# A state-space stage's small matmuls in groups of a few, with dense steps between the groups

## The chip, the cores and the metric

The kernel runs on one core of a Trainium2 chip. The metric is device time in microseconds (us), as the median of several executions. The engines are PE (TensorE: matmuls, with PEld for its weight loads), DVE (VectorE), ACT (ScalarE), POOL (GpSimd) and SP (SyncE, which here issues most transfers). Each engine works through its own list in order.

## What is computed

One layer of a decoder: four token mixers work on the same projection of the input, each is projected up to 1024 channels, gated and summed, and an output projection, a norm, an MLP and a second norm follow. The part that matters here is the state-space mixer (S5) and how it joins the sum:

```python
def _s5_mixer(u, ...):
    bu_re = jnp.einsum('bsgh,gph->bsgp', ug, bb_re)      # and bu_im
    _, _, x_re, x_im = lax.associative_scan(combine, (a_re, a_im, bu_re, bu_im), axis=1)
    y = (jnp.einsum('bsgp,ghp->bsgh', x_re, c_re) - jnp.einsum('bsgp,ghp->bsgh', x_im, c_im)
         + d * ug)
    y = jax.nn.gelu(y.reshape(bsz, s, BRANCH_WIDTH))
    return y * jax.nn.sigmoid(y @ glu_w + glu_b)

branches = (y_s5, y_fox, y_rwkv, y_sb)
merged = sum(jax.nn.sigmoid(gates[:, :, n]) * (branches[n] @ w_branch[i, n])
             for n in range(N_BRANCHES))
```

There are 1024 tokens, 1024 channels and 256 channels for each mixer; S5 has 16 groups of 16 channels with 64 complex states each.

## The kernel before

All large products are done in a split float32 (a high and a low part of each operand): a **dense step** is three matmuls of 128x512, `a*xh`, `a*xl` and `b*xh`, after which the function `dense` yields. Eight steps make one tile of a gate, two make one of a branch's up-projection. The steps of the gates and up-projections of all four branches stand one behind the other in the generator `merges`, in the order RWKV, FoX, S5, stick-breaking. I call it the dense stream; its tiles are named `mm` in the rows. While it runs, the FoX, S5 and stick-breaking mixers are computed one after the other as processes beside it (`attn`, `s5_tables` with `s5`, `attn` again); their PSUM tiles are named `x`.

PE's order is fixed when the program is built. `Driver.run` keeps a modelled time. In each round it lets a process whose time has come run up to its next `yield`, and only when none is due does it take the next step of the dense stream:

```python
ready = [p for p in self.procs if p[0] <= self.now]
if ready:
    ...
    p[0] = self.now + 0.2 if lat is None else self.mark + lat
    continue
if fill is not None:
    got = next(fill, "end")
```

So everything that a process gives to PE between two yields stands in one piece, and after a yield at least one dense step (0.645 us in that model) comes before the process goes on. Where the dense stream needs a branch that isn't finished, it answers "wait", and PE has only what the processes give. DVE's and ACT's lists are put in the order of the modelled times; SP's follows the order in which the code issues.

The S5 stage gives PE these pieces. In `s5_tables`: 16 small products `bd,Gm` (called L here; 128x32, each two matmul instructions), then 16 transposes `cst,Gm` into four PSUM tiles (GT). In `s5`, for each of two halves (`p4`): 32 products `U,GT`; a chain on DVE that ends in the state `X` (its two parts are written one after the other); then the Y products, for eight groups of channels one `U,Tg` and two `X,Hm` each (six matmul instructions of 128 columns), into two PSUM tiles, with a gelu on ACT and DVE after each tile. At the end, `yt` is read back from DRAM, eight products `yt,gw` are done, and the result (`ynat`) goes through ACT and DVE to DRAM (`scr_Y`). From there the dense stream loads it back as the operand `y` (four loads `wr<-scr_Y`, a cast on ACT and a subtraction on DVE for each), and the first step of the S5 branch's up-projection, `mm<-y`, reads it. The weights for that step are a chunk `wr<-in_w_branch`, cast by ACT to `vh`, with the rest `vl` from DVE. The stick-breaking stage begins when S5 has finished; it loads `raw` and `st` tiles on SP, and its first matmuls on PE are transposes `cst,st` and products `KH,QS`; its first transposes `cst,W` follow after a chain on ACT and DVE.

Of the kernel before, what the change touches and what calls it, by code (L numbers as in the profile page):

```python
# [316 lines left out]
def body(ctx, tc, I, O, dbg=None):  # L317
# [25 lines left out]
    def nm(s):  # L343
        uid[0] += 1
        return f"{s}_{uid[0]}"
# [15 lines left out]
    def px():  # L361
        return ps.tile([P, 512], F32, tag="x", name=nm("x"), bufs=5)
# [282 lines left out]
    def rwkv(pool, wa, g1, have, late, spare):  # L645
# [246 lines left out]
        def chain():  # L892
            St = pool.tile([P, 2, 64], F32, tag="St", name=nm("St"), bufs=3)
            V.memset(St, 0.0)
            for qt in range(4):
# [7 lines left out]
                for c_ in range(4):  # L903
# [13 lines left out]
                    yield 0.1  # L917
                    U = px()
                    for ct, hh, hd, hp in heads:
                        js = slice(hd * 64, hd * 64 + 64)  # L920
                        T.matmul(U[up, js], lhsT=TT[up, hd * 2 + c_ // 2, :], rhs=Xs[up, js], start=True, stop=True)
                    A.copy(VU[up, c_, :], U[up, 0:256])
                    V.tensor_tensor(out=sd, in0=St, in1=ec[:, :, c_:c_ + 1].to_broadcast([P, 2, 64]), op=ALU.mult)
# [219 lines left out]
    def tt(o, a, b, op):  # L1143
        V.tensor_tensor(out=o, in0=a, in1=b, op=op)
        return o
# [12 lines left out]
    def cmul(orr, oi, ar, ai, br, bi, tmpf):  # L1158
        a, b = tmpf(), tmpf()
        tt(a, ar, br, ALU.mult)  # L1160
        tt(b, ai, bi, ALU.mult)
        tt(orr, a, b, ALU.subtract)
        a, b = tmpf(), tmpf()
        tt(a, ar, bi, ALU.mult)
        tt(b, ai, br, ALU.mult)
        tt(oi, a, b, ALU.add)
# [103 lines left out]
    def s5_tables(pool):  # L1270
        pw, fr, fi = s5v["pw"], s5v["fr"], s5v["fi"]

        def small(shape, name):
            return pool.tile(shape, F32, tag="s2k", name=nm(name), bufs=4)
        bc_in = small([P, 4, 8, 16], "bcin")
        SY.dma_start(out=bc_in, in_=I["s5_bc"])
        br, bi, cr, ci = (bc_in[:, i] for i in range(4))
        dsb = small([P, 256], "dsb")
        G.dma_start(out=dsb, in_=I["s5_d"].partition_broadcast(P))
        zz = small([112, 256], "zz")  # L1280
        G.memset(zz, 0.0)
        SY.dma_start(out=SCR["L"][128:240], in_=zz)

        def t1k(shape=(P, 8, 8, 16)):
            return pool.tile(list(shape), F32, tag="t1k", name=nm("t1k"), bufs=2)
        E = pool.tile([P, 2, P, 8], F32, tag="E", name="E", bufs=1)
        V.memset(E[:, 0, 0, :], 1.0)
        V.memset(E[:, 1, 0, :], 0.0)

        def grow(k):  # L1290
            n = 1 << k
            bcs = [x.unsqueeze(1).to_broadcast([P, n, 8]) for x in s5v["steps"][k]]
            cmul(E[:, 0, n:2 * n, :], E[:, 1, n:2 * n, :], E[:, 0, 0:n, :], E[:, 1, 0:n, :], bcs[0], bcs[1],
                 lambda: t1k((P, 64, 8))[:, :n, :])

        def b16(a):
            return a.unsqueeze(2).to_broadcast([P, 8, 16])
        bb = pool.tile([P, 2, 8, 16], F32, tag="bb", name="bb", bufs=1)

        def t128():  # L1300
            return pool.tile([P, 8, 16], F32, tag="t128", name=nm("t128"), bufs=4)
        for k in range(5):
            grow(k)
            if k % 2:
                yield 0.1
        cmul(bb[:, 0], bb[:, 1], b16(fr), b16(fi), br, bi, t128)
        nci = pool.tile([P, 8, 16], F32, tag="nci", name="nci", bufs=1)
        ts(nci, ci, -1.0, ALU.mult)
        bd = pool.tile([P, 2, 8, 2, 16], F32, tag="bd", name="bd", bufs=1)
        G.memset(bd, 0.0)  # L1310
        for e in range(2):
            es = slice(e * 64, e * 64 + 64)
            for i, w in ((0, cr), (1, nci)):
                A.copy(bd[es, i, :, e, :], w[es])
        yield 0.1
        pwp = pw.rearrange("p i j a -> p i a j")
        Gm = pool.tile([P, 2, 8, 8, 16], F32, tag="a", name="Gm", bufs=1)
        Hm = pool.tile([P, 2, 8, 8, 16], F32, tag="Hm", name="Hm", bufs=1)

        def bj(a):  # L1320
            return a.unsqueeze(3).to_broadcast([P, 8, 8, 16])

        def bh(a):
            return a.unsqueeze(2).to_broadcast([P, 8, 8, 16])
        prev = [pwp[:, i, :, 7::-1] for i in range(2)]
        pnx = [pwp[:, i, :, 1:9] for i in range(2)]
        cmul(Gm[:, 0], Gm[:, 1], bj(prev[0]), bj(prev[1]), bh(bb[:, 0]), bh(bb[:, 1]), t1k)
        yield 0.1
        lo = px()
        for pr in range(8):  # L1330
            for i in range(2):
                T.matmul(lo[:, pr * 32:pr * 32 + 32], lhsT=Gm[:, i, pr].rearrange("p s h -> p (s h)"),
                         rhs=bd[:, i, pr].rearrange("p e h -> p (e h)"), start=i == 0, stop=i == 1)
        Ls = small([P, 256], "Ls")
        tt(Ls.rearrange("p (g h) -> p g h", h=16), dsb.rearrange("p (g h) -> p g h", h=16),
           cc("eye7").unsqueeze(1).to_broadcast([P, 16, 16]), ALU.mult)
        tt(Ls, Ls, lo[:, 0:256], ALU.add)
        SY.dma_start(out=SCR["L"][0:128], in_=Ls)
        GT = pool.tile([P, 2, 8, P], F32, tag="GT", name="GT", bufs=1)
        for i in range(2):  # L1340
            for p4 in range(2):
                o = px()
                for j in range(4):
                    T.transpose(o[:, j * P:(j + 1) * P], Gm[:, i, p4 * 4 + j].rearrange("p s h -> p (s h)"), ident)
                A.copy(GT[:, i, p4 * 4:p4 * 4 + 4, :].rearrange("p a b -> p (a b)"), o)
        U = pool.tile([P, 16, P], F32, tag="a", name="U", bufs=1)
        for s in range(8):
            SY.dma_start(out=U[s * 16:(s + 1) * 16], in_=SCR["u"].rearrange("(g h) s c -> s h g c", h=16)[s])
        a1, a2 = t1k(), t1k()
        tt(a1, bj(pnx[0]), bh(cr), ALU.mult)  # L1350
        tt(a2, bj(pnx[1]), bh(ci), ALU.mult)
        tt(Hm[:, 0], a1, a2, ALU.subtract)
        yield 0.1
        a1, a2 = t1k(), t1k()
        tt(a1, bj(pnx[0]), bh(nci), ALU.mult)
        tt(a2, bj(pnx[1]), bh(cr), ALU.mult)
        tt(Hm[:, 1], a1, a2, ALU.subtract)
        Tg = pool.tile([P, 16, 8, 16], F32, tag="Tg", name="Tg", bufs=1)
        for s in range(0, 8, 2):
            Tz = small([P, 2, 256], "Tz")  # L1360
            for i in range(2):
                SY.dma_start(out=Tz[:, i, :], in_=SCR["L"][(7 - s - i) * 16:(7 - s - i) * 16 + 128])
            A.copy(Tg[:, :, s:s + 2, :], Tz.rearrange("p s (g h) -> p g s h", h=16))
        for k in range(5, 7):
            grow(k)
            yield 0.1
        yield from s5(pool, GT, Tg.rearrange("p g s h -> p g (s h)"), Hm.rearrange("p i a s h -> p i a (s h)"),
                      E.rearrange("p i j a -> p i a j"), U)

    def s5(pool, GT_, Tg_, Hm_, E_, U_):  # L1370
        def tt(o, a, b, op):
            V.tensor_tensor(out=o, in0=a, in1=b, op=op)
# [7 lines left out]
        for p4 in range(2):  # L1380
            a4 = slice(p4 * 4, p4 * 4 + 4)
            GT, Hm, Ev = GT_[:, :, a4], Hm_[:, :, a4], E_[:, :, a4]
            Tg, U = Tg_[:, p4 * 8:p4 * 8 + 8], U_[:, p4 * 8:p4 * 8 + 8]
            Z = pool.tile([P, 2, 4, P], F32, tag="t1k", name=nm("Z"), bufs=2)
# [33 lines left out]
            for g4 in range(2):  # L1418
                o = px()
                for j in range(4):  # L1420
                    g = j * 2 + g4
                    pr, es = g // 2, slice((g % 2) * 64, (g % 2) * 64 + 64)
                    os_ = o[:, j * P:(j + 1) * P]
                    T.matmul(os_, lhsT=Tg[:, g], rhs=U[:, g, :], start=True, stop=False)
                    for i in range(2):
                        T.matmul(os_, lhsT=Hm[es, i, pr], rhs=X[es, i, pr, :], start=False, stop=i == 1)
                w = pool.tile([P, 512], F32, tag="s2k", name=nm("gl"), bufs=4)
                A.activation(out=w, in_=o, func=AF.Square)
                V.tensor_scalar(out=w, in0=w, scalar1=0.044715, scalar2=1.0, op0=ALU.mult, op1=ALU.add)
                tt(w, o, w, ALU.mult)  # L1430
                A.activation(out=w, in_=w, func=AF.Tanh, scale=math.sqrt(2.0 / math.pi))
                V.scalar_tensor_tensor(out=Ye[:, g4], in0=w.rearrange("p (a b) -> p a b", b=P), scalar=1.0,
                                       in1=o.rearrange("p (a b) -> p a b", b=P), op0=ALU.add, op1=ALU.mult)
# [818 lines left out]
```

## Time and profile before

| what | value |
|---|---|
| median of 3 executions | 1868.21 us (1867.77 to 1874.67) |
| the profiled execution | 1875.13 us, its span 1873.3 us |
| PE busy | 1816.4 us, 97% |
| DVE busy | 1237.8 us, 66% |
| ACT busy | 714.3 us, 38% |
| mean granted TensorE clock | 0.983 |

The span goes from the first to the last instruction; the execution's own time is 1.8 us longer. Busy PE means that some matmul is under way, at either of its two clock levels (2.4 GHz, shown as 1.00, and 1.2 GHz, shown as 0.50), so a busy share of 97% doesn't tell at which speed.

### The profile page before, as it was taken

What the parts mean: (1) busy time and instruction counts of PE and PEld (TensorE: products, weight loads), DVE (VectorE), ACT (ScalarE), POOL (GpSimd) and SP (SyncE); (2) the same over time, 40 slices, a digit from 0 to 9 for tenths busy, and PEclk for the clock granted to TensorE, in tenths of its full rate; (3) what the DMA queues carried; (4) which work ended last, traced back from release to release, by engine and by line L of the source; (5) the groups of instructions that cost most, each with busy time, mean ns of one, the idle gap of its engine ahead of it and who ended that gap; (6) DMA issues with size and microseconds to landing.
All of it is one profiled execution on the core that took longest, in us unless ns stands there. A gap on an engine that the chain in (4) does not pass through costs nothing. (4 is left out here: it accounts for less than half of the span.)

```text
span 1873.3 us, 27588 instructions
## 1 busy us (share of the span) xinstructions
PE 1816.4 (97%) x9651; PEld 1479.0 (79%) x9651; DVE 1237.8 (66%) x2596; ACT 714.3 (38%) x1412; POOL 206.9 (11%) x279
## 2 busy tenths in 40 slices
PE   8999999998999999999999998999999999999998
PEld 6877777777788877777877886788888887888876
DVE  7675855616876765688867667666656565866574
ACT  5443343215554212555544125343333343433230
POOL 0331111100000000000000001111121111111000
PEclk9999999999999988999999999999999999999999
DMA  7334223124422411412155118898989898988441
GB/s 254 108 123 112 76 81 95 63 69 139 146 90 78 104 38 50 137 54 67 44 197 160 62 57 234 239 254 223 255 235 251 212 268 256 284 212 229 127 147 48
DMA packets 178012, 275.27 MB, mean 147 GB/s; under 512 B 37824, under 2 KB 59616, under 8 KB 177744
## 3 DMA queue, kind: packets, MB, share of 16 engines
q1 hardware_dynamic: 155552, 226.31, 37.3%
q0 software_dynamic: 22320, 47.18, 12.8%
q8 instruction: 76, 1.25, 0.3%
q14 instruction: 64, 0.52, 0.1%
HBM read 199.76 MB, written 56.89 MB: 137 GB/s over the span
## 5 line engine op out<-in xcount | busy, mean ns | idle before, releaser
L327 PE MATMUL mm<-t,wh 128*128 128x512 f32 x1600 | 514.3, 403 | 3.8 <-ACT th L280 1.9
L327 PEld LDWEIGHTS mm<-t,wh 128*128 128x128 f32 x1600 | 293.8, 190 | 66.5 <-issue 2.4
L327 PE MATMUL mm<-t,wl 128*128 128x512 f32 x800 | 314.9, 394 | 0.0
L327 PE MATMUL x<-t,wp 128*128 128x512 f32 x1152 | 270.8, 394 | 14.1 <-DVE wp L280 6.8
L327 PEld LDWEIGHTS x<-t,wp 128*128 128x128 f32 x1152 | 217.7, 190 | 64.3 <-DVE wp L280 9.9
L327 PE MATMUL x<-sx,wp 128*128 128x512 f32 x768 | 179.6, 389 | 0.2 <-DVE wp L280 0.2
L327 PEld LDWEIGHTS mm<-t,wl 128*128 128x128 f32 x800 | 151.8, 190 | 33.4
L327 PEld LDWEIGHTS x<-sx,wp 128*128 128x128 f32 x768 | 144.1, 188 | 30.5 <-DVE wp L280 0.7
L280 ACT CAST wh<-wr 128x512 fp32r<-128x512 f32 (+1 forms) x125 | 74.5, 596 | 123.1 <-PE mm L327 90.7
L280 DVE TENSOR_TENSOR wp<-wr,wp 128x512 fp32r<-128x512 f32 x96 | 65.8, 687 | 77.2 <-ACT wp L280 77.2
L280 ACT CAST wp<-wr 128x512 fp32r<-128x512 f32 x96 | 59.1, 620 | 147.8 <-DMA wr<-wl 69.3
L280 POOL TENSOR_TENSOR wl<-wr,wh 128x512 fp32r<-128x512 f32 x50 | 67.7, 1353 | 280.6 <-ACT wh L280 280.4
L327 PE MATMUL mm<-t,wp 128*128 128x512 f32 x384 | 90.6, 392 | 0.0
L327 PE MATMUL mm<-sx,wp 128*128 128x512 f32 x384 | 89.6, 389 | 0.0
L327 PE MATMUL mm<-wo,t 128*128 128x512 f32 x384 | 89.0, 391 | 0.0
L327 PEld LDWEIGHTS mm<-t,wp 128*128 128x128 f32 x384 | 72.6, 189 | 15.6 <-DVE wp L280 0.4
L327 PEld LDWEIGHTS mm<-sx,wp 128*128 128x128 f32 x384 | 72.1, 188 | 14.9
L327 PEld LDWEIGHTS mm<-wo,t 128*128 128x128 f32 x384 | 71.6, 188 | 14.5
L280 DVE TENSOR_TENSOR wl<-wr,wh 128x512 fp32r<-128x512 f32 (+1 forms) x75 | 47.3, 633 | 40.4 <-ACT wh L280 39.5
L280 DVE TENSOR_TENSOR wp<-wl,wp 128x512 fp32r<-128x512 f32 x64 | 43.7, 687 | 42.5 <-ACT wp L280 42.5
L280 DVE TENSOR_TENSOR wp<-wh,wp 128x512 fp32r<-128x512 f32 x64 | 43.9, 689 | 33.7 <-ACT wp L280 33.7
L280 ACT CAST wp<-wl 128x512 fp32r<-128x512 f32 x64 | 39.3, 620 | 50.0 <-DMA wl<-wr 16.5
(380 smaller groups left out, 3199.4 us busy)
## 6 DMA issues: line engine op xcount, KB each, us to landing
wr<-in_w_in_dram SPq DMA_DIRECT2D x110, 256.0 KB
scr_H<-sn SPq DMA_DIRECT2D x100, 256.0 KB
wr<-in_mlp_w_dram SPq DMA_DIRECT2D x84, 256.0 KB
sn<-scr_H SPq DMA_DIRECT2D x84, 256.0 KB
wh<-in_mlp_w_dram SPq DMA_DIRECT2D x56, 256.0 KB
wl<-in_mlp_w_dram SPq DMA_DIRECT2D x56, 256.0 KB
wr<-wl POOLq DMA_DIRECT2D x32, 256.0 KB, 6.5
wl<-wr POOLq DMA_DIRECT2D x32, 256.0 KB, 4.7
```

What stands on the lines that cost most here:

```text
L280: r = f(*a, **kw)
L327: return nc.tensor.matmul(out, lhsT=lhsT, rhs=rhs, **kw)
```

## The change

Three bare `yield None` are added: one after each of the eight pairs of L products, one after each of the four tiles of GT transposes, and one after each group of Y products.

```diff
@@ s5_tables
             for i in range(2):
                 T.matmul(lo[:, pr * 32:pr * 32 + 32], lhsT=Gm[:, i, pr].rearrange("p s h -> p (s h)"),
                          rhs=bd[:, i, pr].rearrange("p e h -> p (e h)"), start=i == 0, stop=i == 1)
+            yield None
         Ls = small([P, 256], "Ls")
@@ s5_tables
                     T.transpose(o[:, j * P:(j + 1) * P], Gm[:, i, p4 * 4 + j].rearrange("p s h -> p (s h)"), ident)
                 A.copy(GT[:, i, p4 * 4:p4 * 4 + 4, :].rearrange("p a b -> p (a b)"), o)
+                yield None
         U = pool.tile([P, 16, P], F32, tag="a", name="U", bufs=1)
@@ s5
                     T.matmul(os_, lhsT=Tg[:, g], rhs=U[:, g, :], start=True, stop=False)
                     for i in range(2):
                         T.matmul(os_, lhsT=Hm[es, i, pr], rhs=X[es, i, pr, :], start=False, stop=i == 1)
+                    yield None
                 w = pool.tile([P, 512], F32, tag="s2k", name=nm("gl"), bufs=4)
```

The dense stream itself keeps its order and its number of steps. What moves is where the S5 and stick-breaking pieces stand in it.

PE at the first half's Y products, before. The row in front is the last dense matmul; each group is one `U,Tg` and a row of two `X,Hm`, and six more groups follow without anything between:

```order
L327 MATMUL mm_7256<-y_6598,vh_7122 128x512
L327 MATMUL mm_7256<-y_6597,vl_7123 128x512
L327 MATMUL x_7263<-U,Tg 128x128
L327 MATMUL x_7263<-X_7147,Hm 128x128 x2
L327 MATMUL x_7263<-U,Tg 128x128
L327 MATMUL x_7263<-X_7147,Hm 128x128 x2
```

The same place in the change:

```order
L327 MATMUL mm_7277<-t_121,wl_7179 128x512
L327 MATMUL x_7302<-U,Tg 128x128
L327 MATMUL x_7302<-X_7174,Hm 128x128 x2
L327 MATMUL mm_7308<-t_107,wh_7126 128x512
L327 MATMUL mm_7308<-t_106,wh_7126 128x512
L327 MATMUL mm_7308<-t_107,wl_7127 128x512
L327 MATMUL x_7302<-U,Tg 128x128
L327 MATMUL x_7302<-X_7174,Hm 128x128 x2
```

One dense step now stands behind each group. The 16 dense steps between the `U,GT` products and the first group are 16 as before, in both halves. At L and GT it is the same: before, 32 L instructions and 16 transposes in one piece; in the change, one dense step behind each two L products and behind each four transposes.

PE behind the `yt,gw` products, before. The place is where the dense stream comes to the S5 branch's `y`, 30 dense steps behind the last `yt,gw`, with the first `KH,QS` products of the stick-breaking stage ahead of it:

```order
L327 MATMUL x_7888<-KL_7683,QS_7681 128x384
L327 MATMUL mm_7822<-t_121,wh_7702 128x512
L327 MATMUL mm_7822<-t_120,wh_7702 128x512
L327 MATMUL mm_7822<-t_121,wl_7703 128x512
L327 MATMUL mm_7904<-y_7733,vh_7803 128x512
L327 MATMUL mm_7904<-y_7734,vh_7803 128x512
```

In the change this place is 7 dense steps behind the last `yt,gw`, ahead of the first `KH,QS` products:

```order
L327 MATMUL mm_7701<-t_121,wh_7638 128x512
L327 MATMUL mm_7701<-t_120,wh_7638 128x512
L327 MATMUL mm_7701<-t_121,wl_7639 128x512
L332 MATMUL x_7802<-cst,st_7773 128x64 x4
L327 MATMUL mm_7830<-y_7794,vh_7824 128x512
L327 MATMUL mm_7830<-y_7795,vh_7824 128x512
```

Of the dense steps that stood behind `yt,gw`, 23 have moved ahead of it.

SP at the same place in the change, from the second store of the S5 result to the weight chunk (`wr_7800`) from which `vh_7824` is made:

```order
L280 DMA scr_Y<-ynat_7730 128x1024
L280 DMA st_7915<-scr_qk 64x512 x2
L280 DMA wr_7760<-scr_Y 128x512
L280 DMA wr_7762<-scr_Y 128x512
L280 DMA st_7775<-scr_qk 64x512
L280 DMA raw_7777<-scr_qk 64x512 x2
L280 DMA raw_7780<-scr_qk 64x512 x2
L280 DMA raw_7783<-scr_qk 64x512 x2
L280 DMA wr_7800<-in_w_branch_dram 128x256
```

The order of kinds is nearly that of before: there, the second of the two late `y` loads stood behind the `raw` loads, and the weight chunk behind that.

## Rows read from the trace of the kernel before

**Rows 1.** This is the page of the profiled execution: its span; the busy time and its share of the span for each engine; and the TensorE clock that was granted in 40 equal slices of the span (46.8 us each, in tenths of full speed).

```profile
span 1873.3 us, 27588 instructions
...
PE 1816.4 (97%) x9651; PEld 1479.0 (79%) x9651; DVE 1237.8 (66%) x2596; ACT 714.3 (38%) x1412; POOL 206.9 (11%) x279
...
PEclk9999999999999988999999999999999999999999
```

**Rows 2.** This is the table of stretches. Columns: from:to in us from the span's start and its length; busy us and (x instructions) of PE, PEld, DVE, ACT and POOL; the mean granted clock (1.00 is 2.4 GHz, 0.50 is 1.2 GHz); the share of the DMA engines; GB/s. 404 to 421 is the RWKV stage with its own small matmuls, 424.5 to 434.6 a place where PE stood still, the other six lie in the state-space stage.

```profile
404.00:421.00 17.00, 17.00 (x135) 12.26 (x134) 2.35 (x9) 1.89 (x4) 0.00 (x0) 1.00 0.12 44
424.50:434.60 10.10, 5.32 (x15) 4.41 (x16) 5.52 (x14) 2.83 (x5) 0.00 (x0) 0.66 0.22 80
626.25:633.60 7.35, 7.35 (x50) 7.34 (x48) 3.64 (x6) 1.64 (x3) 0.00 (x0) 0.70 0.05 18
633.60:636.16 2.56, 2.56 (x9) 2.03 (x7) 2.03 (x4) 1.52 (x4) 0.00 (x0) 0.54 0.44 102
677.73:693.38 15.65, 14.28 (x49) 10.73 (x48) 5.69 (x9) 1.23 (x2) 0.00 (x0) 0.58 0.03 8
693.38:697.38 4.00, 4.00 (x10) 3.14 (x10) 2.80 (x6) 2.04 (x4) 0.00 (x0) 0.50 0.14 43
712.47:725.99 13.52, 12.12 (x49) 9.08 (x47) 7.95 (x13) 1.23 (x2) 0.00 (x0) 0.70 0.18 51
725.99:731.28 5.29, 5.29 (x14) 4.13 (x13) 1.80 (x3) 1.23 (x2) 0.00 (x0) 0.50 0.36 109
```

**Rows 3.** This is PE in order of time, from the L matmuls (`bd,Gm`) over the GT transposes (`cst,Gm`) to the first dense steps behind them (the third matmul of each step is left out). Columns here and below: start us, us taken, engine, line, op, out<-in, shapes, xcount, and in brackets the idle time just before, with what ended it. A matmul's us overlap with those of the next, so a pitch is read from one start to the next.

```profile
626.25 4.23 PE L327 MATMUL x<-bd,Gm 128*128 128x32 f32 x32
630.29 3.65 PE L332 MATMUL x<-cst,Gm 128*128 128x128 f32 x16
633.60 1.20 PE L327 MATMUL mm<-t,wh 128*128 128x512 f32 x2
...
635.02 1.05 PE L327 MATMUL mm<-t,wh 128*128 128x512 f32 x2
...
636.16 0.62 PE L327 MATMUL mm<-t,wh 128*128 128x512 f32 x2
...
636.85 0.62 PE L327 MATMUL mm<-t,wh 128*128 128x512 f32 x2
```

**Rows 4.** This is PE in order of time, the first of the two stretches of Y matmuls (`U,Tg` and `X,Hm`): the wait in its first group, and the start of the next two groups.

```profile
679.90 0.46 PE L327 MATMUL x<-X,Hm 64*128 64x128 f32 x2 [1.38 <-DVE X L280]
680.28 0.78 PE L327 MATMUL x<-U,Tg 128*128 128x128 f32 x2
...
682.14 0.79 PE L327 MATMUL x<-U,Tg 128*128 128x128 f32 x2
```

**Rows 5.** This is PE in order of time, the same three places of the second stretch of Y matmuls.

```profile
714.67 0.46 PE L327 MATMUL x<-X,Hm 64*128 64x128 f32 x2 [1.40 <-DVE X L280]
715.06 0.49 PE L327 MATMUL x<-U,Tg 128*128 128x128 f32 x2
...
716.12 0.49 PE L327 MATMUL x<-U,Tg 128*128 128x128 f32 x2
```

**Rows 6.** This is PE in order of time, two places at full clock: eight transposes of the FoX stage and the dense step behind them, and the dense step behind the small matmuls of the first half's `U,GT`.

```profile
563.61 1.03 PE L332 MATMUL x<-cst,W 128*128 128x128 f32 x8
564.40 0.71 PE L327 MATMUL mm<-t,wh 128*128 128x512 f32 x2
...
666.71 0.73 PE L327 MATMUL mm<-t,wh 128*128 128x512 f32 x2
667.29 0.39 PE L327 MATMUL mm<-t,wl 128*128 128x512 f32 x1
```

**Rows 7.** This is PE in order of time, the end of the state-space stage and the start of the stick-breaking stage: the `yt,gw` matmuls, the dense stream behind them, the first dense step that reads the state-space branch (`mm<-y`), and the first rows with waits after it.

```profile
745.04 7.03 PE L327 MATMUL x<-yt,gw 128*128 128x512 f32 x16
751.50 1.03 PE L327 MATMUL mm<-t,wh 128*128 128x512 f32 x2
...
775.27 0.62 PE L327 MATMUL mm<-y,vh 128*128 128x512 f32 x2
...
780.06 0.73 PE L327 MATMUL mm<-t,wh 128*128 128x512 f32 x2 [1.90 <-ACT th L280]
...
784.71 0.98 PE L332 MATMUL x<-cst,W 128*128 128x128 f32 x7 [0.98 <-DVE W L280]
```

**Rows 8.** This is the SP queue (issues of transfers) in order of time, same stretch; us is the time the issue itself took.

```profile
754.59 0.80 SPq L280 DMA_DIRECT2D wr<-scr_Y  x2
758.24 0.32 SPq L280 DMA_DIRECT2D scr_Y<-ynat  x1
760.93 0.32 SPq L280 DMA_DIRECT2D wr<-scr_Y  x1
761.29 0.47 SPq L280 DMA_DIRECT2D st<-scr_qk  x1
761.87 3.73 SPq L280 DMA_DIRECT2D raw<-scr_qk  x6
...
769.18 0.53 SPq L280 DMA_DIRECT2D wr<-in_w_in_dram  x1
```

**Rows 9.** This is ACT in order of time, same stretch: the last evacuation of the state-space stage, and a cast of a dense weight chunk that waited for its transfer.

```profile
757.08 1.13 ACT L280 ACTIVATE ynat<-yf 128x512 f32<-128x512 f32 x1 [0.28 <-DVE yf L280]
...
771.57 0.62 ACT L280 CAST wh<-wr 128x512 fp32r<-128x512 f32 x1 [0.31 <-DMA wr<-in_w_in_dram]
```

## The prediction

> **What bounds the kernel now.** I read the page first. PE is busy for 97% of the span, so no other engine can be the bound for long, and a change can pay only by making PE's work shorter or by taking waits out of it [rows 1]. A busy PE isn't a PE at full speed, so the clock line came next: it shows an 8 in the 14th and 15th slices alone, which are the state-space stage. The table of stretches says how low it went there [rows 2]. With two levels, 1.00 and 0.50, a mean clock c means that (1.00 - c) / 0.50 of the stretch was at the low one. L and GT (626.25 to 633.60) had 0.70: 60% of 7.35, or 4.4 us. The first Y stretch had 0.58: 84% of 15.65, or 13.1 us, so the clock fell about 2.5 us in, just behind the wait of 1.38 us for `X` [rows 4]. The second had 0.70: 60% of 13.52, or 8.1 us. It was still full for the first 5.4 us, so it lived through a wait of 1.40 us [rows 5] and fell only after some 3.2 us more of small matmuls alone. At L, PE hadn't stood still at all [rows 3]. So two things come ahead of a fall here: a run of small matmuls only, and a short wait beside small matmuls. Behind each of the three, the dense stream goes on at half speed, for 2.56, 4.00 and 5.29 us, until it has run by itself for that long. In the RWKV stage, where small matmuls also stand between other work, 17 us went by at 1.00.
>
> **The gain at the three places, if the clock holds.** A dense step at full clock takes 0.69 us (636.16 to 636.85); at the low one two steps took 2.56 (633.60 to 636.16), so 1.28 each [rows 3]. By that the 4.00 and 5.29 us behind the Y groups are three and four steps (the counts in the table take in matmuls that reach over an end). Each turn from small matmuls to dense costs something of its own: behind small matmuls the third matmul of a step came 0.58 us after its first (666.71 to 667.29, [rows 6]), where two thirds of a 0.69 us step are 0.46, so 0.12 for a turn. The change adds 11 turns at L and GT, 7 in each half of Y.
>
> - L and GT: the transposes took 3.31 us (630.29 to 633.60); at full clock one takes 0.10 (eight in 0.79, [rows 6]), so 1.6: 1.7 saved. The two dense steps behind took 2.56 instead of 2 x 0.69 + 0.12 = 1.5: 1.1 saved. Eleven turns cost 1.3. Sum: 1.5 gained.
> - First Y: from 680.28 to 693.38, 13.1 us for seven groups. At full clock a group takes 1.06 (715.06 to 716.12, [rows 5]) against 1.86 here (680.28 to 682.14, [rows 4]): 7.4, so 5.7 saved. Behind it three steps took 4.00 instead of 3 x 0.69 + 0.12 = 2.2: 1.8 saved. Seven turns cost 0.8. Sum: 6.7.
> - Second Y: from 715.06 to 725.99, 10.9 instead of 7.4: 3.5; behind it four steps in 5.29 instead of 2.9: 2.4; turns 0.8. Sum: 5.1.
>
> Together 13.3 us, if the clock holds everywhere.
>
> **What is moved, and what it costs.** The dense stream has the same steps, so a step that stands between the groups is missing later. The order shows where: 23 steps have gone ahead of `yt,gw`, and the first `mm<-y` comes 7 steps behind the last `yt,gw` and not 30. Before, those 30 were the cover for the way of S5's result through DRAM: `mm<-y` began at 775.27, 23.8 us behind the end of `yt,gw`, and didn't wait [rows 7]. How long is that way? From the start of `yt,gw` (745.04): the last `ynat` ends at 758.21, 13.2 us on, or 12.7 with one ACT operation less ahead of it [rows 9]. Its store to the load behind it took 2.7 (758.24 to 760.93), the issues of loads and `st` some 1.6, the six `raw` issues 3.73 [rows 8]. The weight chunk for `vh` is issued behind all those, so at about 20.5; from a chunk's issue to the cast that waited for it were 2.4 (769.18 to 771.57, [rows 8, 9]), and the cast with its end takes 0.4: `mm<-y` can start at about 23.3. PE gets there after `yt,gw` (6.46), seven steps (4.8), a turn and four small transposes (0.5): at 11.8. So PE stands for **about 11.5 us**, and what is queued behind it on PE is all the rest, dense steps and first stick-breaking products alike. Bounds: 8, if the chunk is loaded early after all and only the late `y` loads count (15.4 + 0.8 for the issues + 2.4 + 1.2 for cast and rest, near 20); 13 if the loads crowd each other; 0 only if the way were hidden, for which no row speaks.
>
> After a stop of that kind the clock is low: around the nearest long wait (424.5 to 434.6) the mean was 0.66 [rows 2]. Four dense steps at half speed cost 4 x 0.6 = 2.4 more (0 if it has come back by then; 3.4 at the most: at 0.66, 68% of the 10.1 us there, 6.9, were low, and half of them is lost). In return two waits of before that lay behind `mm<-y`, 1.90 for `th` and 0.98 for `W` [rows 7], find ACT and DVE caught up after an 11 us stop of PE: 2.9 gained (0 if they move along with it).
>
> Sum without any fall: -13.3 + 11.5 + 2.4 - 2.9 = **-2.3 us**. The gain at the Y groups is to a large part time that is given back at `mm<-y`.
>
> **Does the clock hold?** At L and GT I think it does: the longest piece without dense steps becomes four transposes. At Y I am not sure. The 1.4 us wait for `X` stays, since between the `U,GT` products and the first group there are 16 dense steps as before, and DVE's chain for `X` is the same. It stands in the first group, and row for row PE does the same as before up to the end of that group. In those rows the clock fell once out of two times, in the first half, and lived on in the second. A fall has a worse price in the change than it seems. Once it is low, each group with its step is 1.86 + 1.28 = 3.1 us, of which only 1.25 are dense, and the rows show the clock to come back only after 2.56 to 5.29 us of dense steps without a break. So I expect it to stay low to the end of the groups: 7 x (0.80 + 0.56) = 9.5, and 1.8 more for the dense steps behind, 11.3 us for each half in which it falls. All of it is on the path, since PE is the bound, and S5's result is later by as much while the cover behind `yt,gw` isn't larger.
>
> The Trainium skill has a rule that speaks against the change: "TensorE: Matmul & The Clock Gate", section "A second HAM failure mode: psum-queue depth-cycling", says that a PE which stands still for a moment between groups of matmuls often enough swings between its clock levels, and pays at each turn. By that rule both halves would fall, and the time would be that of the third case below. The RWKV stretch at 1.00 [rows 2] doesn't agree with it as it stands; the fall behind the 1.38 us wait does.
>
> **The rivals.**
> - *No fall.* For it: the second half lived through the wait, and in the change dense steps follow 1.1 us later. Against: the first half fell behind the same wait. 1868.2 - 2.3 = 1865.9. With the bounds of the wait and the restart, 1861 to 1869.
> - *One fall, in either half.* -2.3 + 11.3 = +9.0: 1877.2. If it comes back in the midst of the groups, about 5 less: 1873; if the wait for `y` is at its upper bound with the higher restart, 1881.
> - *Both fall.* +20.3: 1888.5.
> - *Faster, the other side:* the clock holds, and the wait for `y` is short, because the loads of `y` and the weight chunk land early. This decides from a wait of under 4 us: then there is no long stop and no restart at low clock, and -13.3 + 2 to 4, with none or a part of the 2.9, gives about 1858. Against it stand rows 8: the last store's landing and the six `raw` issues lie between `ynat` and the chunk.
> - *The change does nothing to the clock*, because single dense steps are too little in all three places: the L place stays low too, some 4 us more than with both fallen (1.5 not gained, 11 steps at 1.28 in part): up to 1893.
>
> **How the numbers follow.** The sum was made as a difference in the profiled execution (1875.1 us, 6.9 over the median of the three, [rows 1] for its span); I apply it to the median of 1868.2, as differences at these places don't hang on where the 6.9 lie. One fall of two is what the rows of before show for the same piece of work, and a median over executions, whose falls may differ, is drawn to this middle case: 0.43. No fall 0.27; both 0.13; faster with a short wait 0.12; nothing at the clock, 0.05. The likeliest is one fall: **1877 us**, its own range 1873 to 1881. From 1858 to 1889 leaves out most of the case with the short wait and half of the two highest, about 2 in 10. A measurement here tells about 0.5% (9.3 us) from no change: faster than 1858.9 is the short wait, and a little of no fall, 0.13; slower than 1877.5 is over half of one fall with the two highest, 0.38; within, the rest of one fall and nearly all of no fall, 0.49.
>
> **What the profile of the changed kernel would show.** The stretch of L and GT at 1.00, its transposes in fours of 0.4 us. In each half of Y either a pitch of a group with its step of about 1.9 us at 1.00, or about 3.1 at 0.50 up to the last group: how many of each decides between the first three cases. A wait of 8 to 13 us in front of the first `mm<-y`, ended by ACT or DVE (`vh`, `vl`, or the parts of `y`), with clock 0.50 just behind it. The waits of 1.90 and 0.98 gone or under 0.5. The start of `yt,gw` near 748 without a fall (745.04, and 23 steps are 15.9 us more, less 13.3), near 759 with one. I would be wrong above all if the weight chunk was loaded ahead of the `raw` tiles in time (no wait, much faster), if the clock came back inside the groups at once (a fall then costs 2 to 4 us, not 11), or if the clock fell elsewhere, where the order is as before.

## The result, and the profile after

The change is slower: 1894.72 us as the median of 4 executions (1887.15 to 1900.18), against 1871.13 us for four of the kernel before on the same chip. The ratio is 1.0124, with a 95% interval from 1.0094 to 1.0154. I had forecast 1877 us, with a range up to 1889, so the time lies outside. One execution was profiled, the one of 1887.15 us, and five more later (below). Its page, in the lines that answer to [rows 1]:

```profile
span 1885.4 us, 27592 instructions
...
PE 1816.9 (96%) x9651; PEld 1478.4 (78%) x9651; DVE 1238.2 (66%) x2596; ACT 714.3 (38%) x1412; POOL 207.4 (11%) x279
...
PEclk9999999999999979899999999999999999999999
```

The low clock has moved from two slices into the 15th (7) and 17th (8), and PE's busy time is that of before: 12 us more of the span are waits. The table of stretches (columns as in [rows 2]) tells them apart: L and GT with their steps, the first and the second stretch of Y, the stop in front of `mm<-y` and the 6.85 us behind it, and 6.5 us behind a later stop.

```profile
626.54:640.20 13.66, 13.66 (x86) 11.91 (x85) 3.42 (x7) 3.69 (x7) 0.00 (x0) 1.00 0.26 86
680.41:705.10 24.69, 23.27 (x73) 17.71 (x72) 8.52 (x15) 2.94 (x5) 0.00 (x0) 0.59 0.08 27
723.97:740.23 16.26, 14.23 (x74) 11.09 (x73) 8.81 (x15) 2.75 (x5) 0.00 (x0) 1.00 0.03 7
767.85:780.55 12.70, 0.23 (x4) 0.09 (x2) 3.69 (x8) 5.03 (x9) 0.17 (x3) 0.60 0.67 215
780.55:787.40 6.85, 6.84 (x18) 5.01 (x19) 4.38 (x8) 4.25 (x7) 0.00 (x0) 0.50 0.41 136
821.92:828.40 6.48, 6.47 (x18) 5.10 (x19) 1.24 (x3) 0.97 (x2) 0.10 (x1) 0.50 0.14 43
```

L and GT are at 1.00. One half of Y is low and takes 24.7 us, the other is at 1.00 and takes 16.3. The rows of PE that answer to [rows 4, 5, 7] show the pitch of a group with its step (3.15 us in the first half, 1.75 in the second), the waits for `X` in the first group of each half, and the two stops:

```profile
682.58 0.46 PE L327 MATMUL x<-X,Hm 64*128 64x128 f32 x2 [1.37 <-DVE X L280]
...
686.18 0.63 PE L327 MATMUL x<-U,Tg 128*128 128x128 f32 x2
...
689.33 0.63 PE L327 MATMUL x<-U,Tg 128*128 128x128 f32 x2
...
726.79 0.46 PE L327 MATMUL x<-X,Hm 64*128 64x128 f32 x2 [2.03 <-DVE X L280]
...
729.73 0.38 PE L327 MATMUL x<-U,Tg 128*128 128x128 f32 x2
...
731.48 0.38 PE L327 MATMUL x<-U,Tg 128*128 128x128 f32 x2
...
755.89 7.03 PE L327 MATMUL x<-yt,gw 128*128 128x512 f32 x16
...
780.55 1.22 PE L327 MATMUL mm<-y,vh 128*128 128x512 f32 x2 [12.48 <-ACT vh L280]
...
821.92 0.69 PE L332 MATMUL x<-cst,st 64*128 64x64 f32 x4 [3.62 <-DMA st<-scr_qk]
```

What the stop at 780.55 waits for stands in the queues of SP and ACT, as forecast from [rows 8, 9]: the last two loads of `y`, the six `raw` issues, and only then the weight chunk, whose cast `vh` PE waits for.

```profile
771.98 0.80 SPq L280 DMA_DIRECT2D wr<-scr_Y  x2
772.89 0.45 SPq L280 DMA_DIRECT2D st<-scr_qk  x1
773.39 3.82 SPq L280 DMA_DIRECT2D raw<-scr_qk  x6
777.31 0.53 SPq L280 DMA_DIRECT2D wr<-in_w_branch_dram  x1
```

```profile
780.10 0.40 ACT L280 CAST vh<-wr 128x256 fp32r<-128x256 f32 x1 [0.87 <-DMA wr<-in_w_branch_dram]
```

To follow the time I compare the same place in both traces. At the start of `yt,gw` the change is 10.85 us later (755.89 to 745.04, [rows 7]), with 23 more steps done, which are 15.7 us: so 4.8 us ahead. Deep in the stick-breaking stage, where PE's order is the same again, this row of PE is in the trace of before, and behind it the one of the change:

```profile
899.57 0.63 PE L327 MATMUL mm<-y,vh 128*128 128x512 f32 x2
```

```profile
914.05 0.62 PE L327 MATMUL mm<-y,vh 128*128 128x512 f32 x2
```

There it is 14.5 us late. So 19.3 us were lost between `yt,gw` and that row: 12.48 and 3.62 of waits, and half of the two low stretches (3.4 and 3.2), together 22.7, less the two waits of before, which mostly went (1.90 and 0.98). By the end of the span 2.4 of the 14.5 are gone: from that row on the change took 971.3 us, the profile of before 973.8, and a second profile of before (below) 971.6, so this is no more than executions differ by.

### The profile page after: what moved, and what is told of

It reads as the page before. It is cut to its first block, busy times and chain, and to the rows that moved or that the text cites. A ratio compares the mean times of both kernels' runs of the same rounds, so it can differ in the third digit from the quotient of the medians.

```text
span 1885.4 us, 27592 instructions
## 1 busy us (share of the span) xinstructions
PE 1816.9 (96%) x9651; PEld 1478.4 (78%) x9651; DVE 1238.2 (66%) x2596; ACT 714.3 (38%) x1412; POOL 207.4 (11%) x279
## 5 line engine op out<-in xcount | busy, mean ns | idle before, releaser
L327 PEld LDWEIGHTS mm<-wo,t 128*128 128x128 f32 x384 | 71.6, 188 | 14.5
L327 PE MATMUL mm<-y,vh 128*128 128x512 f32 x176 | 59.2, 419 | 12.7 <-ACT vh L280 12.5
```

The costliest lines, as they stand in the source:

```text
L327: return nc.tensor.matmul(out, lhsT=lhsT, rhs=rhs, **kw)
```

## Experiments

The time of the kernel before is the median on the same chip, taken together with the runs: 1868.56 us for the first four runs, 1864.54 for the next four, 1868.19 for the four after those, and a single execution of 1875.60 for the last three.

**Each part alone.** First only the steps of L and GT (the `yield` in Y is taken out of the change), then only those of Y (the two in `s5_tables` are taken out):

```diff
                         T.matmul(os_, lhsT=Hm[es, i, pr], rhs=X[es, i, pr, :], start=False, stop=i == 1)
-                    yield None
```

> Only the steps between the L products and the GT transposes are kept; the Y groups stand in one piece as before. 23 dense steps are left behind the last yt,gw, instead of 30 before and 7 in the change. My theory (the loss is a stop in front of mm<-y when the cover behind yt,gw is used up, and falls of the clock in the Y groups): L and GT at a granted clock of 1.00 and some 1.5 us gained there, a wait of 0 to 1.5 us in front of mm<-y, no later stop of several us on st, so a time within 4 us of before (1867 to 1874). The rival (each step put between small matmuls costs by itself, 23.6 us for 28 places, so 0.84 a place): 12 places cost 10 us, about 1881.

> Only the steps between the Y groups are kept; L and GT stand in one piece as before. 16 dense steps are left behind the last yt,gw. My theory: a wait of some 6.5 us in front of mm<-y (24.2 us of way, less 6.5 for yt,gw, 11.1 for 16 steps and 0.5), low clock behind it, and a half of Y in which the clock has fallen stays low to its last group at a pitch of 3.15 us. One half fallen gives about 1885, both about 1896. The rival (0.84 us a place, 16 places): 1884 whatever the clock does, and no wait of more than 2 us in front of mm<-y.

L and GT alone took 1875.4 us (ratio 1.0047, 1.0025 to 1.0068), Y alone 1884.94 (1.0103, 1.0076 to 1.0131). Stretches of L and GT and of the second Y of the first kernel, with a row of PE just ahead of the latter:

```profile
625.10:638.70 13.60, 13.60 (x85) 11.89 (x84) 3.42 (x7) 3.63 (x7) 0.00 (x0) 1.00 0.27 84
...
716.30:732.00 15.70, 15.70 (x51) 12.02 (x50) 3.34 (x7) 1.83 (x3) 0.00 (x0) 0.50 0.17 47
```

```profile
714.85 1.22 PE L327 MATMUL mm<-t,wh 128*128 128x512 f32 x2 [3.83 <-DVE th L280]
```

L and GT are at 1.00 and `mm<-y` waits only 0.55 us, as my theory had it, but the gain isn't in the time. The 12 steps have shifted the dense stream against DVE's chain for `X`: a step just ahead of the Y groups waits 3.83 us for `th`, the evacuation of a finished branch tile, on the engine that does that chain, and the groups behind are low throughout (the first half is low in part, as before: 0.64 from 678.98 to 692.00). I hadn't looked for that wait. Of the second kernel, the two stretches of Y, the row of PE ahead of the second, and the stop:

```profile
675.40:690.30 14.90, 13.52 (x71) 10.48 (x69) 7.92 (x13) 2.16 (x4) 0.00 (x0) 1.00 0.14 44
711.60:735.00 23.40, 23.40 (x70) 17.92 (x68) 4.60 (x8) 3.01 (x5) 0.00 (x0) 0.51 0.07 24
```

```profile
710.80 0.73 PE L327 MATMUL mm<-t,wh 128*128 128x512 f32 x2 [3.83 <-DVE th L280]
...
778.13 1.22 PE L327 MATMUL mm<-y,vh 128*128 128x512 f32 x2 [6.10 <-ACT vh L280]
```

With 16 steps of cover instead of 7 the stop is 6.10 us instead of 12.48 (6.5 expected): 9 steps fewer cost 6.4 us, 0.7 each, which is a step's own time. One half fell here too, this time the second, behind the same wait for `th` as in the first kernel. The times alone don't refute the rival (about 1881 and 1884 us expected, 1875.4 and 1884.94 measured); the stop of 6.10 us does, for which the rival allowed 2 at most, and so does the next run.

**The cover alone.** The kernel before, with a delay only:

```diff
             yt.append(y_)
-        yield 0.1
+        yield 15.0
```

> The kernel before, with no step between small matmuls at all; a delay in front of the yt,gw products (15 us by the builder's reckoning) moves the same 23 dense steps ahead of them as the change does, and PE's order behind them is that of the change, row for row at the start: seven steps, four transposes, mm<-y. My theory (the cover behind yt,gw is what is paid with): the wait of 12 to 13 us in front of mm<-y, low clock behind it and the stop on st of some 3.6 us are there as in the change, and the time is 18 to 23 us over before (by the two traces, PE lost 23.4 us between the start of yt,gw and the first products of the stick-breaking stage). The rival (the loss is in the steps between small matmuls): within 6 us of before.

1886.67 us, ratio 1.0118 (1.0079 to 1.0156). PE in order of time:

```profile
756.07 7.03 PE L327 MATMUL x<-yt,gw 128*128 128x512 f32 x16
...
781.06 1.22 PE L327 MATMUL mm<-y,vh 128*128 128x512 f32 x2 [12.79 <-ACT vh L280]
...
823.05 0.69 PE L332 MATMUL x<-cst,st 64*128 64x64 f32 x4 [4.18 <-DMA st<-scr_qk]
```

No step stands between small matmuls, and both stops are there as in the change. So what is lost is the cover: 18.5 us, by the ratios nearly the whole difference. What the change does to the clock is the remainder, small in the medians and of either sign.

**The cover given back from elsewhere, and a shorter way for y.** The change with a stored gate tile of the stick-breaking branch (16 steps) moved from behind the S5 branch to ahead of it; and the change with the stick-breaking loads started later (the `yield 7.0`):

```diff
-    G0, GS = 5, (3, 1, 0, 1)
+    G0, GS = 5, (3, 1, 1, 0)
...
+            if not fox:
+                yield 7.0
             while jobs and (tag or jobs[0][0] == 0):
```

> The whole change, and 16 dense steps (one stored gate tile of the stick-breaking branch) are moved in the dense stream from behind the S5 branch to just ahead of it: 23 steps stand behind the last yt,gw instead of 7. My theory: the wait of 12.5 us in front of mm<-y shrinks to 1 or 2 us, the low clock behind it and the later stop on st go too, and the time is 15 to 20 us under the change, 1875 to 1880. The rival (the stop only shows that PE has too little to do, and the 16 steps are missing later as a wait of the same size): within 4 us of the change, 1891 to 1898, with a new wait of some 10 us where the stick-breaking stage ends.

> The whole change, and the stick-breaking stage starts its loads 7 us later by the builder's reckoning, so that SP issues the weight chunk for vh ahead of the six raw loads. By the sum of the prediction those issues (3.7 to 3.9 us) are a part of the way of S5's result: the wait in front of mm<-y falls from 12.5 to about 8.3 us. If the stick-breaking chain isn't the bound behind it, the time is some 4 us under the change, 1884 to 1893; if it is, the 4 us come back as waits for st, KL or W in that stage, and the time is that of the change within 2 us.

The first took 1888.11 us (1.0113, 1.0097 to 1.0129), the second 1901.42 (1.0173, 1.0146 to 1.0200). Rows of PE of the first, with the cast on ACT that ends its later wait, then rows of PE of the second:

```profile
786.13 0.73 PE L327 MATMUL mm<-y,vh 128*128 128x512 f32 x2 [0.76 <-ACT vh L280]
...
973.53 1.22 PE L327 MATMUL mm<-y,wh 128*128 128x512 f32 x2 [11.29 <-ACT wh L280]
```

```profile
973.08 0.41 ACT L280 CAST wh<-wr 128x256 fp32r<-128x256 f32 x1 [8.20 <-DMA wr<-in_w_branch_dram]
```

```profile
776.94 1.22 PE L327 MATMUL mm<-y,vh 128*128 128x512 f32 x2 [9.95 <-ACT vh L280]
...
915.04 0.43 PE L332 MATMUL x<-cst,st 64*128 64x64 f32 x4 [2.70 <-DMA st<-scr_qk]
...
977.04 1.22 PE L327 MATMUL mm<-y,wh 128*128 128x512 f32 x2 [4.33 <-ACT wh L280]
```

Both shortened the stop, to 0.76 and 9.95 us, and in both the time came back later: the 16 steps, 11 us, were the cover of the stick-breaking branch's own way through DRAM, and 11.29 us is what PE waits there now, for a weight chunk that SP issues behind the loads of that branch's `y`. Of the two expectations the rival's mechanism held for the first, though with a time between the two. The second is slower than either of its expectations (1884 to 1893, or within 2 us of the change) and has the highest ratio of all runs; beside the waits shown, one of 3.68 us for `wh` follows at 985.23. By these runs the dense steps are a stock that just covers the chain from S5 through the stick-breaking stage, and a step spent early is missing later.

**The wait for X.** The change, with 4 more steps ahead of the first Y group of each half:

```diff
             Ye = Y.rearrange("p (a e) c -> p e a c", e=2)
-            yield 0.1
+            yield 2.7
```

> The whole change, and the Y groups begin 2.6 us later by the builder's reckoning, so that some 4 more dense steps stand ahead of the first group of each half and X is ready when PE comes to it. No step is left behind yt,gw. If the short wait for X is what brings the clock down: no wait in the first groups, both halves at 1.00 with a pitch of 1.75 us, 11 us gained for each half that fell in the change, and a wait of 17 to 18 us in front of mm<-y instead of 12.5: 1875 to 1886. The rival (small matmuls in groups with steps between pull the clock down by themselves, with or without a wait): a fall in at least one half as before, and the longer wait on top: 1896 or more.

1882.06 us (1.0073, 1.0048 to 1.0099). Both stretches of Y, then rows of PE ahead of the first and at the stop:

```profile
685.80:699.50 13.70, 13.70 (x71) 10.73 (x70) 3.88 (x6) 2.45 (x5) 0.00 (x0) 0.98 0.04 11
721.40:734.80 13.40, 13.40 (x71) 10.55 (x70) 4.91 (x9) 2.59 (x5) 0.00 (x0) 1.00 0.01 1
```

```profile
681.53 0.73 PE L327 MATMUL mm<-t,wh 128*128 128x512 f32 x2 [2.51 <-DVE th L280]
...
774.97 1.22 PE L327 MATMUL mm<-y,vh 128*128 128x512 f32 x2 [17.22 <-ACT vh L280]
```

Without a wait in the first group both halves held, and all four executions had a mean clock of 0.985 or 0.986, where those of the change had 0.974 to 0.982. By the ratios it is half a per cent under the change (the intervals just meet), although its stop is 4.7 us longer. The waits haven't gone altogether: one of 2.51 us for `th` now stands in the dense stream, 4.2 us ahead of the first half. With that much dense work between wait and groups the clock held; that it is the steps between the groups that hold it isn't shown, since no version without them had the wait taken away. Even so the version is slower than before.

**How many halves fall.** The change itself five times more, and the kernel before once more, each with a profile:

> The change itself, for another execution's profile. My theory: times fall in groups some 8 to 11 us apart, by the number of halves of Y in which the clock fell. At a time near 1887 one half has a pitch of 3.15 us and the other 1.75; near 1895 or more both have 3.15 up to the last group. The rival: the pitch pattern is that of the first profile (one half low) whatever the time, and the difference lies in another stage.

> The change itself, a third execution's profile. Two were profiled, at 1887.15 and 1885.07 us, each with one half of Y at 0.50 to its last group. If this one is at 1893 us or more, both halves have a pitch of 3.15 us; if it is near 1886, one has.

> The change itself. At 1893 us or more: both halves of Y at a pitch of 3.15 us. Near 1886: one. If it is at 1893 us or more with one half low, the slower group has another cause.

> The change itself, a further execution. At 1893 us or more: both halves of Y at a pitch of 3.15 us. Near 1886: one half. Near 1876: none.

> The change itself, a further execution, with the same three cases: none, one or both halves of Y low, some 9 to 11 us apart.

> The kernel before itself, for another execution's profile. The one profiled first took 1875.1 us and was low in all three stretches (L, and both of Y); most executions take 1865 to 1870. My theory: at such a time one of the three stretches is at or near 1.00, or low for some us less, so that the profile first shown had more to gain than the median, by about the 6.9 us between them. The rival: all three are as low as before, and the difference lies elsewhere (the MLP, or waits).

The change took 1885.07, 1883.96, 1882.79, 1889.44 and 1894.86 us. The first four have one half low and the other at 1.00, like the profile shown above; the last has both low. Where one half fell, it was the first in three profiles and the second in two. Stretches of the execution of 1882.79 us, then of that of 1894.86:

```profile
678.00:701.00 23.00, 21.57 (x70) 16.48 (x69) 7.96 (x13) 2.34 (x4) 0.00 (x0) 0.60 0.10 29
721.60:737.20 15.60, 13.57 (x71) 10.52 (x69) 8.79 (x14) 2.15 (x4) 0.00 (x0) 1.00 0.00 1
```

```profile
679.30:702.60 23.30, 21.86 (x70) 16.70 (x68) 7.91 (x13) 2.34 (x4) 0.00 (x0) 0.59 0.09 29
722.90:746.50 23.60, 21.57 (x70) 16.58 (x68) 8.71 (x13) 2.15 (x4) 0.00 (x0) 0.61 0.00 1
```

So the slower group, to which three of the first four executions belong by their time and mean clock (0.974 to 0.976), is that of two falls. None of six profiles has none. The kernel before took 1861.67 us in its second profile. Its L and GT and its two stretches of Y, to be read beside [rows 2]:

```profile
624.40:631.60 7.20, 7.20 (x51) 7.16 (x50) 3.89 (x6) 1.85 (x4) 0.00 (x0) 0.76 0.05 18
674.30:688.50 14.20, 12.85 (x50) 9.72 (x49) 5.64 (x9) 1.32 (x3) 0.00 (x0) 0.66 0.03 9
707.50:717.20 9.70, 8.31 (x48) 6.31 (x47) 7.96 (x13) 1.23 (x2) 0.00 (x0) 1.00 0.21 68
```

The second stretch is at 1.00 without any step in it, 13.5 us under the execution that the prediction was made from. The loss in all three stretches, from which the forecast gain was made, was that of a bad execution: here L, GT and the first half are low for a shorter time and the second not at all.

**Fewer steps.** Steps only where they might be worth it: one behind each four pairs of L and each second group of Y (8 places); the L steps alone (2); and the eight with 1.4 us more ahead of each half's first group.

```diff
+            if pr in (3, 7):
+                yield None
...
+                    if j == 1 or (j, g4) == (3, 0):
+                        yield None
```

> Few steps instead of many: none behind the GT transposes, one behind each four pairs of L products (2 places), one behind each second group of Y but the last of a half (3 places in each half), 8 places where the change has 28. 24 dense steps are left behind the last yt,gw. My theory (a step there is worth its place only as far as it holds the clock, and costs cover behind yt,gw otherwise): L and GT at 1.00 or nearly, a wait of under 1.5 us in front of mm<-y, no later stop of several us on st. With the clock held in both halves about 1861, with one fall about 1870. The rival (each step within the S5 stage costs, about 0.84 us a place whatever the clock does): 1868.6 + 6.7, about 1875. If single steps between pairs of groups are too few to hold the clock, both halves are at 0.50 and the time is 1872 or more.

> Two dense steps only, one behind each four pairs of L products; Y in one piece. 28 steps are left behind the last yt,gw. My theory: L and GT at 1.00 (low in both profiles of before for 6.8 and 3.4 us), 1 to 2.5 us gained, no wait in front of mm<-y: 0 to 2.5 us under before. The rival (each place costs 0.84 us): 1.7 us over before. The two differ by less than executions of one kernel do, so only the interval tells.

> The eight steps of the sparse version, and the Y groups begin 1.4 us later by the builder's reckoning: 18 dense steps ahead of each half's first group. 23 steps are left behind the last yt,gw. If the wait for X beside small matmuls is what brings the clock down: no such wait in the first half, which stays at 1.00 in each execution; in the second, a wait of DVE's th among the ten steps behind the FoX branch's steps may come instead, and is harmless where steps follow it. Times then fall in one group at 1858 to 1866 instead of two groups (1865 to 1873, 1883 to 1887). If the clock falls all the same, the two groups stay.

They took 1871.13 us (1.0054, 1.0023 to 1.0085), 1870.37 (1.0007, 0.9981 to 1.0032) and 1869.52 (1.0024, 0.9996 to 1.0053). None beats the kernel before; for the second the interval takes in both the 0 to 2.5 us of gain that I expected and the rival's 1.7 of loss. The eight places split into two groups of times (1865.06 to 1873.27 and 1882.99 to 1886.98). The profiled one, of 1870.52 us, has one half low, for which about 1870 was expected; the 1861 of no fall didn't come. The third version lies at 1861.86 to 1878.26, without the higher group, but not in the one group up to 1866 that I expected. In its profile the first half has no wait and is at 1.00, and the second is low, behind a wait for `th` that I had called harmless. The wait ahead of the second half in the version with eight places (0.53 from 705.50 to 725.00), then the wait and the stretch behind it in the third:

```profile
705.54 0.50 PE L327 MATMUL mm<-t,wl 128*128 128x512 f32 x1 [3.40 <-DVE wl L280]
```

```profile
704.86 0.73 PE L327 MATMUL mm<-t,wh 128*128 128x512 f32 x2 [2.62 <-DVE th L280]
```

```profile
706.50:724.00 17.50, 17.50 (x55) 13.27 (x53) 3.66 (x6) 1.74 (x3) 0.00 (x0) 0.50 0.10 31
```

So the wait for `X` isn't the only one that comes ahead of a fall. In the four profiles in which PE waited 2.6 to 3.8 us for a DVE tile in a dense step at most 1.6 us ahead of the second half, that half was low, with steps between its groups or without. The best execution of the version with the L steps alone, at 1854.21 us, is the clearest look at the clock. Its two stretches of Y, in one piece each as before:

```profile
672.00:681.60 9.60, 8.21 (x47) 6.22 (x46) 7.94 (x13) 1.50 (x3) 0.00 (x0) 1.00 0.23 68
699.20:708.90 9.70, 8.24 (x47) 6.27 (x46) 7.99 (x13) 1.23 (x2) 0.00 (x0) 1.00 0.19 68
```

Both are at 1.00, with waits of 1.39 and 1.46 us for `X` in their first groups.

## Why the prediction was wrong, point by point

- **L and GT hold.** Right: 1.00 in each profile of the change. The gain was under-sized: 10 steps more stand in 13.66 us than in the 7.35 + 2.56 of before [rows 2], so 9.91 - (13.66 - 6.9) = 3.1 us where I had 1.5. I had left the L products out, of which the last 1.2 us (629.10 to 630.29) were low too, at 0.52; that is 0.6 us, and where the other 1.0 lies I can't tell.
- **Y.** The pitches were right: 1.75 with the clock held, 3.15 without (1.9 and 3.1 forecast), and a fallen half stays low to its last group. From the first L product to `yt,gw` the execution of two falls took 140.1 us (625.41 to 765.54), that of 1882.79 us 129.4 (624.17 to 753.56): 10.7 us for the second fall, against 11.3. The start of `yt,gw` in the first profile is 755.89, where I had put it near 759 for one fall. Wrong was that the wait for `X` stays as it was: in the second half it is 2.03 us in place of 1.40.
- **The stop in front of `mm<-y`.** Right in place and cause, and nearly in size: 12.48 us against 11.5 (13 at most), and between 12.7 and 13.1 in the other profiles of the change. A falling cover costs a step's time for each step, as the runs with 16 and 0 steps of cover show (6.10 and 17.22 us). The restart took 6.85 us at 0.50, 3.4 us lost, at the upper bound; I had taken 2.4.
- **What failed first: the waits behind it.** I counted 2.9 us as given back there, and they mostly were. But the sum has no term for a second stop, and there is one, 3.62 us for `st`, with low clock behind it, 3.2 us lost. The delay alone brings it (4.18 us), Y alone has it behind its shorter stop (4.10), and L and GT alone, without a stop, waits 0.59 us for `st`; so it goes with the stop and the new order behind it, in which SP issues that load at 817.85, after it has waited 7.1 us for `KL` and 3.7 for `vl`, both on DVE. I had followed the order only to the first `KH,QS`.
- **What failed next: the base.** I applied a difference that was made in an execution of 1875.1 us to the median of 1868.2, "as differences at these places don't hang on where the 6.9 lie". They do: the second profile of before is 13.5 us shorter, and 9.2 of those lie between the first L product and `yt,gw` (118.8 us against 109.6), in just the stretches that the change was to make faster. No execution at the median itself was profiled. Against its own execution the forecast of one fall is 1875.1 + 9.0 = 1884, and the five executions with one fall took 1882.79 to 1889.44.
- **What failed last: the case.** I gave one fall 0.43 and both 0.13. Of the first four executions three were of the second kind by time and mean clock, of the later five one by its profile. My own sum for both is 1888.5, still inside the range; with the 6.9 us of the base it is 1895.4 (from the 1871.13 us measured beside the change, 1891.4), and 1894.72 was measured. So the fall of both halves took the time out of the likeliest case, and the base took it out of the range. That the first of these sums agrees to a microsecond is luck: the second stop, 6.8 us, was missing from the sum, and against it `yt,gw` came 2.8 us sooner than the sum has it and the end gave 2.4 back.
- **The rivals.** The short wait for `y` and the clock that doesn't react didn't come. By the Trainium skill's rule that I cited ("TensorE: Matmul & The Clock Gate", on the queue that cycles through PSUM) both halves would fall; one execution of six profiled agrees, and the two stretches of the execution of 1854.21 us, at 1.00 with waits in them, don't.

What stays open is what makes a half fall in one execution and not in another: in the profiles of the change PE's rows are the same, in the same order and with the same wait.

## What to carry to other kernels

Where one stream of work fills the waits of a chain of latencies, count it as a stock: a filler step that is put inside the chain lengthens the chain by its own time and is gone from the place where it was the cover. First find the wait that the stock covers last, and how much it has to spare; a faster clock is worth only what is left after that. And before a gain is reckoned from one profile, see whether that execution is a usual one in the very stretches concerned.

## What the runs showed of the hardware

Executions of one program differ by up to 22.6 us, and the mean clock goes with it: the kernel before took 1853.61 us in one execution, at a mean clock of 0.993, and 1876.19 in another on the same chip, at 0.984. The version with the L steps alone had both Y stretches at 1.00 and took 1854.21 us in one execution, at a mean clock of 0.995, and 1862 to 1873 us in the others, at 0.983 to 0.990. Once low, PE stayed at 0.50 to the end of a half of Y, in which small matmuls and dense steps take turns. Behind it and behind the stops, dense steps with little or nothing between them brought the full clock back, within 2.56 to 5.29 us in [rows 2] and within 6.85 and 6.48 us in the change.
